# A third raw tile for seven-product pairs, five weight slots instead of six, and another pairing of the product banks

## The chip, the core and the metric

The kernel runs on one core of a Trainium2 chip. The core's engines that matter here are PE (matrix products into PSUM; its weight loads appear as PEld), DVE (elementwise arithmetic), ACT (copies with a change of type, activations) and SP, whose queue issues nearly all the loads from HBM. Each engine works through its own queue in order and waits there for the others by semaphores. The metric is the device time of one execution in microseconds (us), as the median of several runs.

## The reference: what is computed

A decoder trunk of two layers over 256 tokens of width 2048, all in float32. Each layer is a mixer (layer 0: sliding-window attention beside an mLSTM; layer 1: forgetting attention) and a gated feed-forward network (FFN) of hidden width 5632. The change touches the code that computes the FFN:

```python
def swiglu(xn, w_gate, w_up, w_down):
    return (jax.nn.silu(xn @ w_gate) * (xn @ w_up)) @ w_down
...
        h = h + mix.astype(h.dtype)
        h = h + swiglu(rms_norm(h, norm_ffn[layer]), w_gate[layer], w_up[layer], w_down[layer])
```

## The kernel before

**Precision.** A float32 operand is kept as two float32r tiles, `hi` (a rounded copy) and `lo` (what the copy lost). One product of blocks is then three matmuls into one accumulator, `hi`x`hi`, `lo`x`hi`, `hi`x`lo` (`three`, L563 to L565). Activations are split once; weights stream through once and are split on the way. A split of weights is a cast on ACT (L212, L386) and a subtraction on DVE (L213, L387).

**Pair groups.** `pair_group` (L567) multiplies the 256 tokens (two halves `t0`, `t1` of 128) by 512 columns of two weight matrices, or of two column ranges of one matrix. It walks over pairs of k blocks (a k block is 128 rows). A pair is done in one of two ways:

- *plain*: the two matrices' chunks (two k blocks by 512 columns each) are loaded into raw tiles of a pool of four, split into one **slot** each (a `hi` and a `lo` tile of two blocks), and used in 2 x 2 x 2 = 8 products, 24 matmuls.
- *with seven products* (as in Strassen's scheme): all four weight blocks are loaded into one raw tile of four blocks (tag `quad`, two buffers). Three blocks are split as they are into a **triple** (two of these; L648, 128x1536 elements). Then DVE forms differences inside the raw tile (L651, L654, L655), and these are split into two slots (L657 and L658). Seven products, 21 matmuls, follow (L663 to L669); four of them go into the accumulators `prods[0]` to `prods[3]`, three into the plain accumulators.

`ORDER` has eight pairs, of which the second, fourth and sixth are done with seven products. In the FFN a group makes two slots per pair in either way. `slot()` hands out the entries of `stock`, six slots in rotation; a slot is written again once PE has finished with what was in it.

**PSUM.** In the FFN each of two pools, `pa` and `pm`, has two tiles of two banks (a bank holds 128x512 float32). A group's plain accumulators, `plain[0]` and `plain[1]`, are two tiles of one pool and its four products two tiles of the other. The next group changes the pools over (`par`), so that its plain accumulators take the tiles in which the products of this group were.

**The end of a group.** `combine` (L581) adds up the products: ACT copies `prods[0]` (L583), DVE adds `prods[3]` (L585), `prods[2]` (L586) and `prods[1]` (L587, both results at once). Then DVE adds the plain accumulators (L701), ACT and DVE apply the gate (L703, L705), and the result is transposed, by DMA (L734, L736, L741) or, for the last group of the first part, by PE (L720). The outcome is split and summed for the down projection by the function `join` (L387 with `ml`, L300 to L303). The tile `c` that `combine` writes has one buffer, so L583 has to wait until the `join` of the group before has read it.

**The order.** The FFN runs in three parts of 3, 4 and 4 gate/up groups; each part is followed by two groups of the down projection, which adds up over the parts. The order of instructions within each engine's queue is laid out when the program is built, by a simulated time line (`schedule_with_timeline_sim=True`): weight splits of the next group may stand ahead of the end of this one. A tile's buffer is handed on when the last reader of the whole tile is done.

**Around it.** `close_layer` runs the output projection (`out_proj`), sets up the FFN's tiles, takes the `stock` and runs `ffn`. Outside the FFN `stock` is empty and each `slot()` takes fresh tiles of the pool `wp` (tags `hi` and `lo`, six buffers each).

Of the kernel before, what the change touches and what calls it, by code (L numbers as in the profile page):

```python
# [7 lines left out]
F32 = mybir.dt.float32  # L8
BF16 = mybir.dt.bfloat16
F32R = mybir.dt.float32r  # L10
# [7 lines left out]
P = 128  # L18
# [5 lines left out]
NB = 512  # L24
CK = 2
# [29 lines left out]
QUADS = 2  # L55
# [20 lines left out]
def trunk(  # L76
# [24 lines left out]
    mh = sp_.tile([P, KT, S], F32R, name="mh")  # L101
    ml = sp_.tile([P, KT, S], F32R, name="ml")
    wp = ctx.enter_context(tc.tile_pool(name="wp", bufs=6))
    stock, triples = [], []

    def slot():
        if not stock:
            return [wp.tile([P, CK, NB], F32R, tag=a, name=a) for a in ("hi", "lo")]
        stock.append(stock.pop(0))
        return stock[-1]  # L110

    def triple():
        triples.append(triples.pop(0))
# [104 lines left out]
    def two_banks(par, name):  # L218
        return Acc((pm if par else pa).tile([P, NT, NB], F32, tag="pm" if par else "acc", name=name))
# [347 lines left out]
    def pair_group(fp, par, lhs, sums, mats, order, todo=(), halves=None, inner=None, raws=None):  # L567
        plain = [two_banks(par, "acc") for _ in range(2)]
        begun = set()

        def fresh(*at):
            known = at in begun
            begun.add(at)
            return not known

        todo = list(todo)
        prods = None
        kinds = [kind for kind, _ in order]
        t0, t1 = slice(0, P), slice(P, 2 * P)

        def combine(prods):  # L581
            c = fp.tile([P, 4, NB], F32, tag="c", name="c", bufs=1)
            nc.scalar.copy(c[:, 0, :], prods[0])  # L583
            if halves is None:
                nc.vector.tensor_tensor(out=c[:, 1, :], in0=prods[3], in1=c[:, 0, :], op=ALU.add)  # L585
                nc.vector.tensor_tensor(out=c[:, 2, :], in0=prods[2], in1=c[:, 1, :], op=ALU.add)  # L586
                nc.vector.tensor_tensor(  # L587
                    out=c[:, 1:4:2, :],
                    in0=prods[1].rearrange("p (a n) -> p a n", a=1).broadcast_to([P, 2, NB]),
                    in1=c[:, 1:3, :],  # L590
                    op=ALU.add,
                )
                return c
            nc.vector.tensor_tensor(out=c[:, 2, :], in0=prods[3], in1=c[:, 0, :], op=ALU.add)
            nc.vector.tensor_tensor(out=c[:, 1, :], in0=prods[2], in1=c[:, 2, :], op=ALU.add)
            nc.vector.tensor_tensor(out=c[:, 3, :], in0=prods[1], in1=c[:, 1, :], op=ALU.add)
            nc.vector.tensor_tensor(out=c[:, 2, :], in0=prods[1], in1=c[:, 2, :], op=ALU.add)
            return c

        for pos, (kind, pair) in enumerate(order):  # L600
            k0 = 2 * pair
            if inner is not None and pos == len(order) - 1:
                c = combine(prods)
                inner()
            if not kind:
                last = pos == len(order) - 1
                walk = [(i, t) for i in range(CK) for t in range(NT)]
                if last:
                    walk.sort(key=lambda it: it[1])
                for m, (w, c0) in enumerate(mats):  # L610
                    hi, lo = load_chunk(w, k0, c0, NB)
                    run_due(todo, pos)
                    for i, t in walk:
                        ah, al = lhs(k0 + i)
                        ts = slice(t * P, (t + 1) * P)
                        three(
                            plain[m][t], ah[:, ts], al[:, ts], hi[:, i, :], lo[:, i, :],
                            fresh(m, t), last and i == CK - 1,
                        )
                continue  # L620
            first, last = 1 not in kinds[:pos], 1 not in kinds[pos + 1 :]
            if first:
                if 1 - par and halves:
                    prods = [pm.tile([P, NB], F32, tag="pm", name="prod") for _ in range(4)]
                else:
                    prods = [b for _ in range(2) for b in two_banks(1 - par, "prod")]
            if halves:
                ra, rb = (load_raw(w, k0, c0, NB, fp, W_RAWS, raws) for w, c0 in mats)
                hg, lg = split_chunk(ra, NB)
                run_due(todo, pos)  # L630
                hu, lu = (m[:, 0, :] for m in slot())
                split_plain(hu, lu, rb[:, 0, :])
                nc.vector.tensor_tensor(out=ra[:, 1, :], in0=rb[:, 1, :], in1=ra[:, 1, :], op=ALU.subtract)
                nc.vector.tensor_tensor(out=rb[:, 1, :], in0=rb[:, 1, :], in1=rb[:, 0, :], op=ALU.subtract)
                nc.vector.tensor_tensor(out=rb[:, 0, :], in0=rb[:, 0, :], in1=ra[:, 1, :], op=ALU.subtract)
                nc.vector.tensor_tensor(out=ra[:, 0, :], in0=ra[:, 0, :], in1=rb[:, 0, :], op=ALU.subtract)
                parts = []
                for src in (ra, rb):
                    hs, ls = halves.pop(0)
                    halves.append((hs, ls))  # L640
                    split_plain(hs, ls, src)
                    parts += [(hs[:, b, :], ls[:, b, :]) for b in range(CK)]
            else:
                raw = fp.tile([P, 2 * CK, NB], F32, tag="quad", name="raw", bufs=QUADS)
                for m, (w, c0) in enumerate(mats):
                    load_raw(w, k0, c0, NB, into=raw[:, CK * m : CK * (m + 1), :])
                hg, lg = triple()
                latest[0] = split_plain(hg, lg, raw[:, 0:3, :])  # L648
                hu, lu = hg[:, 2, :], lg[:, 2, :]
                run_due(todo, pos)  # L650
                nc.vector.tensor_tensor(  # L651
                    out=raw[:, 1:4:2, :], in0=raw[:, 3:4, :].broadcast_to([P, 2, NB]), in1=raw[:, 1:3, :], op=ALU.subtract
                )
                nc.vector.tensor_tensor(out=raw[:, 2, :], in0=raw[:, 2, :], in1=raw[:, 1, :], op=ALU.subtract)  # L654
                nc.vector.tensor_tensor(out=raw[:, 0, :], in0=raw[:, 0, :], in1=raw[:, 2, :], op=ALU.subtract)  # L655
                (h1, l1), (h0, l0) = slot(), slot()
                split_plain(h1, l1, raw[:, 1:4:2, :])  # L657
                split_plain(h0, l0, raw[:, 0:3:2, :])  # L658
                parts = [((h0, h1)[b % 2][:, b // 2, :], (l0, l1)[b % 2][:, b // 2, :]) for b in range(4)]
            sh, sl = sums(pair)  # L660
            xa, la = lhs(k0)
            xb, lb = lhs(k0 + 1)
            three(prods[0], xb[:, t0], lb[:, t0], hg[:, 1, :], lg[:, 1, :], first, last)  # L663
            three(plain[0][0], xa[:, t0], la[:, t0], hg[:, 0, :], lg[:, 0, :], fresh(0, 0), False)
            three(plain[1][0], sh[3], sl[3], hu, lu, fresh(1, 0), False)
            three(prods[1], sh[0], sl[0], *parts[1], first, last)
            three(prods[2], sh[2], sl[2], *parts[3], first, last)
            three(prods[3], sh[1], sl[1], *parts[2], first, last)
            three(plain[0][1], xa[:, t1], la[:, t1], *parts[0], fresh(0, 1), False)  # L669
        if inner is None:  # L670
            c = combine(prods)
        return plain, c
# [129 lines left out]
    def close_layer(layer, w_out, idx, key, **rest):  # L802
        with tc.tile_pool(name=f"fp{layer}", bufs=2) as fp:
            junk_of[:] = fp, "tmp", 2
            nx = len(mixed_of(ORDER))
            nd = max(len(mixed_of(o)) for o in DOWN.values())
            sx = [fp.tile([P, nx, 4, P], F32R, name=f"sx{i}", bufs=1) for i in range(2)]
            x4 = fp.tile([P, 2, P], F32R, name="x4", bufs=1)
            todo = out_proj(w_out, idx, key, (*sx, x4, fp))
            sd = [fp.tile([P, nd, 4, P], F32R, tag=f"sd{i}", name=f"sd{i}", bufs=1) for i in range(2)]  # L810
            triples.extend([fp.tile([P, 3, NB], F32R, name=f"{a}{i}", bufs=1) for a in ("hi", "lo")] for i in range(2))
            stock.extend([slot() for _ in range(6)])
            renew_pm(2)
            ffn(layer, fp, sx, x4, sd, key, todo, **rest)
            renew_pm(4)
            stock.clear()
            triples.clear()


    acc0 = new_acc()  # L820
    hi, lo = slot()
# [598 lines left out]
```

## Time and profile before

| | us |
|---|---|
| median of 3 runs | 2149.96 |
| lowest and highest run | 2145.96, 2150.37 |
| the profiled execution | 2147.85 |
| its span, first to last instruction | 2146.1 |
| PE busy | 2088.5 (97%) |
| DVE busy | 1801.8 (84%) |
| ACT busy | 1357.8 (63%) |
| mean granted clock of PE | 0.987 |

In the page's groups a line gives: source line, engine, operation, output<-inputs, shape, count | busy time in all, mean ns of one | idle time of the engine just before such instructions, and what ended it. In the view of waits a line gives who waited for whom: us in all, times, longest. In a time line each row has start and length in us, then, in brackets, how long the engine had been idle and what ended that. In the view of windows a row gives, for a stretch of time, each engine's busy time with its count of instructions, the clock granted to PE as a share of full speed, the busy share of the DMA engines and GB/s.

### The profile page before, as it was taken

The numbers are of one execution on the slowest core, as the hardware profiler recorded it, in microseconds if no ns is written. First come the engines' busy times: TensorE is split into PE (matmuls) and PEld (weight loads), VectorE is DVE, ScalarE is ACT, GpSimd is POOL, SyncE is SP. The second block draws the span as 40 slices with busy tenths as digits, with TensorE's granted clock in tenths as the row PEclk, the third lists the DMA queues.
The fourth block names the chain that finished last, engine by engine and source line by source line (L and its number), as shares of the span: only waits on it lengthen the run. The fifth ranks groups of instructions, "written<-read, shape, count | busy, mean of one in ns | idle before, by whom it ended". The sixth has DMA issues, their size and how long they took to land.

```text
span 2146.1 us, 26428 instructions
## 1 busy us (share of the span) xinstructions
PE 2088.5 (97%) x9473; PEld 1726.3 (80%) x9473; DVE 1801.8 (84%) x2095; ACT 1357.8 (63%) x1649; POOL 40.0 (2%) x69
## 2 busy tenths in 40 slices
PE   9999999989999999999999999999999999999997
PEld 7878887868888888787888887888778878888786
DVE  6788779898898999988798777589988889899884
ACT  6766677654666556566676766686654567456563
POOL 1000000000000000000000000000000000000000
PEclk9999999999999999999999999999999999999999
DMA  8666676666676667665676765576756666667663
GB/s 287 181 188 198 201 242 204 203 199 196 209 219 191 206 206 226 215 189 155 209 221 182 224 212 171 168 236 225 226 168 192 219 188 204 210 193 217 199 194 136
DMA packets 309572, 434.84 MB, mean 203 GB/s; under 512 B 106413, under 2 KB 114625, under 8 KB 309313
## 3 DMA queue, kind: packets, MB, share of 16 engines
q1 hardware_dynamic: 307088, 426.27, 63.4%
q0 software_dynamic: 1632, 5.80, 0.8%
q8 instruction: 74, 1.21, 0.2%
q10 hardware_dynamic: 720, 1.09, 0.1%
q14 instruction: 58, 0.47, 0.1%
HBM read 408.68 MB, written 2.12 MB: 191 GB/s over the span
## 4 chain that ended last, share of the span: by engine, by line
PE 77%; DVE 10%; DMA 5%; issue 4%; ACT 4%; SPq 1%; POOL 0%; ACTq 0%; POOLq 0%; DVEq 0%
PE acc L563 16%; PE acc L564 16%; PE acc L565 16%; PE acc L251 5%; PE acc L250 5%; PE acc L252 5%; PE prod L563 4%; PE prod L564 4%; PE prod L565 4%; DVE lo L213 3%; DVE lo L387 2%; DMA raw<-in_w_down_dram 2%; DMA raw<-in_w_up_dram 1%; ACT hi L386 1%; DVE raw L651 1%
## 5 line engine op out<-in xcount | busy, mean ns | idle before, releaser
L212 ACT CAST hi<-raw 128x1024 fp32r<-128x1024 f32 (+3 forms) x561 | 564.5, 1023 | 316.9 <-PE acc L565 141.9
L213 DVE TENSOR_TENSOR lo<-raw,hi 128x1024 fp32r<-128x1024 f32 (+3 forms) x561 | 658.9, 1185 | 125.3 <-ACT hi L212 124.1
L563 PE MATMUL acc<-hi,xh 128*128 128x512 f32 x1320 | 515.1, 393 | 17.2 <-DVE c L586 15.9
L386 ACT CAST hi<-raw 128x1024 fp32r<-128x1024 f32 (+2 forms) x299 | 345.8, 1167 | 273.7 <-PE acc L565 108.1
L564 PE MATMUL acc<-lo,xh 128*128 128x512 f32 x1320 | 517.1, 392 | 0.0
L565 PE MATMUL acc<-hi,xl 128*128 128x512 f32 x1320 | 515.7, 391 | 0.0
L387 DVE TENSOR_TENSOR lo<-raw,hi 128x1024 fp32r<-128x1024 f32 (+2 forms) x299 | 405.9, 1362 | 112.7 <-ACT hi L386 112.3
L563 PEld LDWEIGHTS acc<-hi,xh 128*128 128x128 f32 x1320 | 249.7, 189 | 71.8 <-issue 19.1
L565 PEld LDWEIGHTS acc<-hi,xl 128*128 128x128 f32 x1320 | 249.7, 189 | 52.4
L564 PEld LDWEIGHTS acc<-lo,xh 128*128 128x128 f32 x1320 | 249.8, 189 | 52.1 <-DVE lo L213 0.2
L563 PE MATMUL acc<-hi,mh 128*128 128x512 f32 x466 | 181.7, 393 | 6.1 <-DVE c L586 5.3
L564 PE MATMUL acc<-lo,mh 128*128 128x512 f32 x466 | 182.5, 392 | 1.1 <-DVE lo L213 1.1
L565 PE MATMUL acc<-hi,ml 128*128 128x512 f32 x466 | 182.1, 391 | 0.0
L250 PE MATMUL acc<-hi,mh 128*128 128x512 f32 (+1 forms) x322 | 126.7, 394 | 4.4 <-DVE c L1273 4.4
L251 PE MATMUL acc<-lo,mh 128*128 128x512 f32 (+1 forms) x322 | 126.0, 391 | 0.0
L252 PE MATMUL acc<-hi,ml 128*128 128x512 f32 (+1 forms) x322 | 125.6, 392 | 0.0
L651 DVE TENSOR_TENSOR raw<-raw 128x1024 f32<-128x1024 f32 x95 | 115.6, 1217 | 0.4
L563 PEld LDWEIGHTS acc<-hi,mh 128*128 128x128 f32 x466 | 88.4, 190 | 25.8 <-issue 6.4
L564 PEld LDWEIGHTS acc<-lo,mh 128*128 128x128 f32 x466 | 88.2, 189 | 20.0 <-DVE lo L213 1.7
L565 PEld LDWEIGHTS acc<-hi,ml 128*128 128x128 f32 x466 | 88.2, 189 | 18.5
L250 PE MATMUL acc<-hi,xh 128*128 128x512 f32 (+3 forms) x288 | 100.0, 347 | 3.0 <-DVE c L1273 1.3
L251 PE MATMUL acc<-lo,xh 128*128 128x512 f32 (+3 forms) x288 | 99.5, 345 | 0.8 <-DVE lo L213 0.6
(356 smaller groups left out, 2935.1 us busy)
## 6 DMA issues: line engine op xcount, KB each, us to landing
raw<-in_w_gate_dram SPq DMA_DIRECT2D x176, 512.0 KB, 4.2
raw<-in_w_up_dram SPq DMA_DIRECT2D x176, 512.0 KB, 4.8
raw<-in_w_down_dram SPq DMA_DIRECT2D x176, 512.0 KB, 4.9
raw<-in_w_in_odd_dram SPq DMA_DIRECT2D x88, 512.0 KB, 4.9
raw<-in_w_in_even_dram SPq DMA_DIRECT2D x51, 512.0 KB, 4.9
raw<-in_w_out_even_dram SPq DMA_DIRECT2D x32, 512.0 KB, 4.8
raw<-in_w_out_odd_dram SPq DMA_DIRECT2D x32, 512.0 KB, 4.2
hr<-in_w_in_even_dram SPq DMA_DIRECT2D x12, 512.0 KB, 4.9
```

The costliest lines, as they stand in the source:

```text
L212: latest[0] = nc.scalar.copy(hi[:, k, 0:n], raw[:, k, 0:n])
L213: nc.vector.tensor_tensor(out=lo[:, k, 0:n], in0=raw[:, k, 0:n], in1=hi[:, k, 0:n].bitcast(F32), op=ALU.subtract)
L250: nc.tensor.matmul(o, ah[:, ts], hi, start=(k == 0), stop=False)
L251: nc.tensor.matmul(o, ah[:, ts], lo, start=False, stop=False)
L252: nc.tensor.matmul(o, al[:, ts], hi, start=False, stop=(k == k_all - 1 and cs.stop == n))
L386: cast = nc.scalar.copy(dst_h, src)
L387: nc.vector.tensor_tensor(out=dst_l, in0=src, in1=dst_h.bitcast(F32), op=ALU.subtract)
L563: nc.tensor.matmul(o, ah, hi, start=start, stop=False)
L564: nc.tensor.matmul(o, ah, lo, start=False, stop=False)
L565: nc.tensor.matmul(o, al, hi, start=False, stop=stop)
L651: nc.vector.tensor_tensor(out=raw[:, 1:4:2, :], in0=raw[:, 3:4, :].broadcast_to([P, 2, NB]), in1=raw[:, 1:3, :], op=ALU.subtract)
```

## The change

It does three things, all in the FFN's pair groups. The stock is five slots in place of six, and the buffer so freed becomes a third raw tile for the pairs with seven products, beside the two of tag `quad`. For that, a slot's `hi` and `lo` become the halves of one tile of `wp`. The three raw tiles are held for the whole FFN and handed out in rotation by `quad()`, starting with the one that comes from `wp`. Lastly, the four products are spread over their two PSUM tiles in another way: `prods[0]` with `prods[3]` and `prods[2]` with `prods[1]`, where it was 0 with 1 and 2 with 3.

```diff
     wp = ctx.enter_context(tc.tile_pool(name="wp", bufs=6))
-    stock, triples = [], []
+    stock, triples, quads = [], [], []
 
     def slot():
         if not stock:
-            return [wp.tile([P, CK, NB], F32R, tag=a, name=a) for a in ("hi", "lo")]
+            both = wp.tile([P, 2, CK, NB], F32R, tag="hi", name="hi")
+            return [both[:, a, :, :] for a in range(2)]
         stock.append(stock.pop(0))
         return stock[-1]
+
+    def quad():
+        quads.append(quads.pop(0))
+        return quads[-1]
...
-                    prods = [b for _ in range(2) for b in two_banks(1 - par, "prod")]
+                    (p0, p3), (p2, p1) = two_banks(1 - par, "prod"), two_banks(1 - par, "prod")
+                    prods = [p0, p1, p2, p3]
...
-                raw = fp.tile([P, 2 * CK, NB], F32, tag="quad", name="raw", bufs=QUADS)
+                raw = quad()
...
-            stock.extend([slot() for _ in range(6)])
+            stock.extend([slot() for _ in range(5)])
+            own = wp.tile([P, 2, CK, NB], F32R, tag="hi", name="raw").rearrange("p a k n -> p (a k) n").bitcast(F32)
+            quads.extend([own] + [fp.tile([P, 2 * CK, NB], F32, tag="quad", name="raw", bufs=QUADS) for _ in range(QUADS)])
             renew_pm(2)
             ffn(layer, fp, sx, x4, sd, key, todo, **rest)
             renew_pm(4)
             stock.clear()
             triples.clear()
+            quads.clear()
```

## The prediction

> **What bounds the kernel now.** I read the page's busy shares first, then what PE waited for, then the time lines around its longest waits.
>
> ```profile
> PE 2088.5 (97%) x9473; PEld 1726.3 (80%) x9473; DVE 1801.8 (84%) x2095; ACT 1357.8 (63%) x1649; POOL 40.0 (2%) x69
> ```
>
> ```profile
> PE acc L563 <- DVE c L586: 21.3, 6, 5.3
> ...
> PE prod L563 <- DVE ml L387: 5.7, 1, 5.7
> ...
> PE acc L563 <- DVE c L587: 1.6, 3, 0.8
> ...
> PE acc L564 <- DVE lo L213: 1.1, 1, 1.1
> ```
>
> PE is the bound, and it is idle for 2146.1 - 2088.5 = 57.6 us. The largest share, 21.3 us, is one kind of wait: the first matmul of a group waits for the addition of `prods[2]` (L586), because its accumulator is the PSUM tile that held that product. Waits for plain splits (L213) hardly occur. The time line of PE has the long waits one by one, each with the last matmul before it:
>
> ```profile
> 479.72 0.79 PE L563 MATMUL prod<-hi,sd 128*128 128x512 f32 x1 [5.67 <-DVE ml L387]
> ...
> 901.38 0.39 PE L565 MATMUL acc<-hi,xl 128*128 128x512 f32 x1
> 906.12 0.77 PE L563 MATMUL acc<-hi,xh 128*128 128x512 f32 x1 [4.36 <-DVE c L586]
> ...
> 1191.20 0.47 PE L250 MATMUL acc<-hi,xh 128*128 128x512 f32 x1 [1.30 <-DVE c L1273]
> ...
> 1545.86 0.39 PE L565 MATMUL acc<-hi,xl 128*128 128x512 f32 x1
> 1551.10 0.77 PE L563 MATMUL acc<-hi,mh 128*128 128x512 f32 x1 [4.85 <-DVE c L586]
> ...
> 1743.29 0.39 PE L565 MATMUL acc<-hi,xl 128*128 128x512 f32 x1
> 1748.98 0.77 PE L563 MATMUL acc<-hi,xh 128*128 128x512 f32 x1 [5.30 <-DVE c L586]
> ...
> 2000.62 0.39 PE L565 MATMUL acc<-hi,xl 128*128 128x512 f32 x1
> 2006.23 0.76 PE L563 MATMUL acc<-hi,xh 128*128 128x512 f32 x1 [5.22 <-DVE c L586]
> ```
>
> A long wait costs more than itself. The view of windows sets a stretch without waits beside the one after the wait that ends at 906.12:
>
> ```profile
> 568.00:611.00 43.00, 43.00 (x192) 35.60 (x190) 41.13 (x44) 28.55 (x29) 0.00 (x0) 1.00 0.74 220
> ...
> 906.00:912.00 6.00, 5.88 (x14) 4.65 (x15) 5.86 (x6) 1.71 (x3) 0.00 (x0) 0.50 0.83 317
> ```
>
> At clock 1.00 a matmul takes 43.00/192 = 0.224 us, afterwards, at clock 0.50, 5.88/14 = 0.42. These 14 slow matmuls cost 14 x 0.196 = 2.7 us. The same rows show DVE at 41.13 of 43 us in a gate group: it has hardly more room than PE. After the wait of 1.30 us the first matmul took 0.47 us, after the four long ones 0.76 to 0.77.
>
> Why is L586 late? Before the wait that ends at 1748.98, in the time lines of SP, ACT and DVE:
>
> ```profile
> 1730.48 0.37 SPq L151 DMA_DIRECT2D raw<-in_w_gate_dram  x1
> 1730.90 0.46 SPq L151 DMA_DIRECT2D raw<-in_w_up_dram  x1
> ```
>
> ```profile
> 1731.48 1.06 ACT L212 CAST hi<-raw 128x1024 fp32r<-128x1024 f32 x1 [0.98 <-PE prod L565]
> 1737.48 1.48 ACT L386 CAST hi<-raw 128x1536 fp32r<-128x1536 f32 x1 [4.95 <-DMA raw<-in_w_up_dram]
> ```
>
> ```profile
> 1729.24 1.21 DVE L387 TENSOR_TENSOR lo<-raw,hi 128x1024 fp32r<-128x1024 f32 x1
> ...
> 1739.00 1.76 DVE L387 TENSOR_TENSOR lo<-raw,hi 128x1536 fp32r<-128x1536 f32 x1 [2.39 <-ACT hi L386]
> ...
> 1744.68 0.68 DVE L585 TENSOR_TENSOR c<-prod,c 128x512 f32<-128x512 f32 x1
> ...
> 1748.15 0.68 DVE L586 TENSOR_TENSOR c<-prod,c 128x512 f32<-128x512 f32 x1
> ...
> 1750.49 1.21 DVE L587 TENSOR_TENSOR c<-prod,c 128x1024 f32<-128x1024 f32 x1
> ```
>
> The split that ends at 1729.24 + 1.21 = 1730.45 is the last reader of a four-block raw tile. Only then do the two loads of the next such tile go out, at 1730.48 and 1730.90. ACT, done with its work at 1732.5, stands 4.95 us before that tile's cast, and DVE is idle for 2.39. What ends the group, L585 to L587, is queued behind on both engines.
>
> **The third raw tile.** It lets this load go out one plain pair and one with seven products earlier (45 matmuls of 0.224, 10 us), so the data is there at 1732.5. The cast also needs a free triple, of which there are still two; I take it as free, since PE had begun the pair that used it. The gain is DVE's idle time. The other places, with their own idle times:
>
> ```profile
> 476.70 1.76 DVE L387 TENSOR_TENSOR lo<-raw,hi 128x1536 fp32r<-128x1536 f32 x1 [2.24 <-ACT hi L386]
> ...
> 896.14 1.76 DVE L387 TENSOR_TENSOR lo<-raw,hi 128x1536 fp32r<-128x1536 f32 x1 [1.81 <-ACT hi L386]
> ...
> 901.83 0.68 DVE L585 TENSOR_TENSOR c<-prod,c 128x512 f32<-128x512 f32 x1
> ...
> 907.64 1.21 DVE L587 TENSOR_TENSOR c<-prod,c 128x1024 f32<-128x1024 f32 x1
> ...
> 1545.13 0.68 DVE L585 TENSOR_TENSOR c<-prod,c 128x512 f32<-128x512 f32 x1
> ...
> 1551.47 1.22 DVE L587 TENSOR_TENSOR c<-prod,c 128x1024 f32<-128x1024 f32 x1
> ...
> 1996.25 1.76 DVE L387 TENSOR_TENSOR lo<-raw,hi 128x1536 fp32r<-128x1536 f32 x1 [2.68 <-ACT hi L386]
> ...
> 2001.93 0.68 DVE L585 TENSOR_TENSOR c<-prod,c 128x512 f32<-128x512 f32 x1
> ...
> 2007.74 1.21 DVE L587 TENSOR_TENSOR c<-prod,c 128x1024 f32<-128x1024 f32 x1
> ```
>
> At 1551 DVE was not idle; I count nothing there from this part. At 479.72 the wait falls from 5.67 to 5.67 - 2.24 = 3.4 us.
>
> **The banks.** The next group's first accumulator now takes the tile of `prods[0]` and `prods[3]`, free after L585. With DVE earlier by its idle time, L585 ends at 902.5 - 1.8 = 900.7, 1545.8, 1745.4 - 2.4 = 1743.0 and 2002.6 - 2.7 = 1999.9, each time before PE's last matmul has ended (at 901.8, 1546.3, 1743.7, 2001.0): the first wait is gone. What is late next is the second tile, free after L587, which PE reaches twelve matmuls (2.7 us) into the group. L587 ends at 908.85 - 1.8 = 907.0, 1552.7, 1751.7 - 2.4 = 1749.3, 2008.95 - 2.7 = 2006.3; PE is there at 904.5, 1549.0, 1746.4, 2003.7. So four waits stay: 2.5, 3.7, 2.9 and 2.6, 11.7 us in place of 4.36 + 4.85 + 5.30 + 5.22 = 19.7. Gain 8.0, and 2.2 at 479.72. The two short waits for L586 turn into waits for L587, at no gain. `prods[1]` moves into the later tile, so a group needs that tile three matmuls (0.7 us) sooner; PE has no wait in the whole view for the additions that free it (L701), so this costs nothing, and at most 0.7 us in each of 33 groups.
>
> The slow matmuls: a wait of 1.30 us leaves the clock up, one of 4.36 does not. By the nearer of the two (the middle is 2.8), the waits of 2.5 and 2.6 keep full speed, and 2.9, 3.7 and 3.4 do not: two stretches go, 2 x 2.7 = 5.5 us.
>
> **Five slots.** ACT's casts already wait for PE to leave a slot:
>
> ```profile
>   PE acc L565: 250.0, 154
> ```
>
> (The line is from the raw tiles' list of what ended idle time of the engine ahead of an instruction: us, times.) With five, each cast may start one chunk of twelve matmuls, 2.7 us, later, and its subtraction after it; behind them in ACT's and DVE's queues stand the next casts and the group's end. As a slot's content is ready several chunks ahead of PE, this is hidden in most groups; with that cover gone, one subtraction more falls behind each gate group's end:
>
> ```profile
> L213 DVE TENSOR_TENSOR lo<-raw,hi 128x1024 fp32r<-128x1024 f32 (+3 forms) x561 | 658.9, 1185 | 125.3 <-ACT hi L212 124.1
> ```
>
> There are 22 gate groups, so the bound is 22 x 1.2 = 26 us. At the long waits the sign can turn: a split that has to wait for its slot can no longer stand ahead of L586. Bounds -5 and 26; I take 3 us, nearer to PE's 1.1 us of waits for L213.
>
> **The rest.** The new raw tile comes from the pool that `out_proj` still uses, and it serves the first such pair of each FFN. If it came free only with `out_proj`'s last matmuls, the load would be late: 6.5 us from the issue at 1730.90 to the cast at 1737.48, and the cast itself 1.48. Bounds 0 and 2 x 8 us; I take 1, since PE comes to that pair only after a plain pair. One tile for `hi` and `lo` holds a `lo` one matmul longer, hidden by the cast that has to precede its next writing; nothing. The loads that move ahead in SP's queue let the plain loads behind them go out sooner; nothing.
>
> **Sum**, against the profiled execution: 2147.85 - 8.0 - 2.2 - 5.5 + 3 + 1 = 2136 us. That execution lies 2 us under the median of the runs, within their spread of 4.4 us, so I predict 2136 without correction. Its own range is 2128 to 2144.
>
> **The clock, weighed.** The Trainium skill (TensorE: Matmul & The Clock Gate, Part 1) says that PE's clock falls to half after an idle window of about 3.4 us. The traced waits of 1.30 and 4.36 us agree, and 0.50 is half.
>
> **Rivals.**
> 1. *The clock stays up after every remaining wait* (what the rule just named makes of waits of 2.5 to 3.7 us; no row shown has a wait between 1.30 and 4.36 to contradict it). Then three more slow stretches go: 2136 - 8 = 2128 us. Chance 0.13.
> 2. *The group's end moves up whole.* L583 stood behind the late cast; without it ACT and DVE can have the combination done before PE ends the group. Then the 19.7 and 5.7 us of waits and all five slow stretches go: 2147.85 - 25.4 - 13.5 + 4 = 2113. Against it: DVE is busy for 41 of 43 us, so work moved up pushes other work back. Chance 0.15.
> 3. *Nothing gained from the raw tile:* the cast waits for its triple instead. Then L587 stays where it was, the second waits are 4.4, 3.7, 5.3 and 5.2, and the gain is 1 us: 2147 plus or minus 3. This is the case in which the change doesn't do what it says. For it: casts do wait for PE's products (0.98 us at 1731.48). Chance 0.12.
> 4. *The slot decides, and it is slower.* In every gate group DVE, with 2 us to spare, loses its lead of one split to ACT's longer waits, and PE meets it: +26 us against a gain of 15.7, so 2147.85 + 10 + 1 = 2159. It decides from 15.7/22 = 0.7 us a gate group on. For it: 250 us of such waits now. Chance 0.27.
>
> **Chances.** My forecast has 0.33. Faster by over 0.2% (4.3 us, what a measurement here can tell): 0.33 + 0.13 + 0.15, less a little for the forecast's upper edge, 0.60. Rival 3 and that edge give 0.12 for within 0.2%, rival 4 gives 0.28. The range is 2108 to 2163: rival 2 with 5 us below it, rival 4 with 4 above.
>
> **What would show it.** Right: the 128x1536 casts no longer idle for a load of a raw tile, the waits for L586 are gone, and waits for L587 of 2 to 4 us stand in their place. Rival 1 shows as clock 1.00 after these; rival 3 as idle time of that cast ended by PE; rival 4 as waits of PE for L213, L387 or the casts, and more than 250 us of casts waiting for PE. A wait at the first seven-product pair after either `out_proj` would show my 1 us wrong.

## The result, and the profile after

| | before | after |
|---|---|---|
| median of 4 runs, us | 2148.28 | 2126.01 |
| lowest and highest run | 2145.96, 2150.37 | 2124.25, 2127.69 |
| ratio, with 95% interval | | 0.9897 (0.9879 to 0.9914) |
| profiled execution, and its span | 2147.85, 2146.1 | 2127.0, 2125.3 |
| mean granted clock of PE | 0.987 | 0.995 |

The change makes the kernel 22 us faster (1.0%). That is inside the whole range, 2108 to 2163, which holds every rival, but beyond the likeliest value, 2136, and 2 us below the range that the forecast itself was given, 2128 to 2144. The executions that were profiled differ by 20.8 us of span. Lines of the code have moved: in the profile of after, L568 to L570 are `three`, L590, L591 and L592 the additions of `prods[3]`, `prods[2]` and `prods[1]`, L217 and L218 the plain splits, L391 and L392 the other splits. A slot's `lo` now has the name `hi`, since both are one tile.

The page's busy times of after:

```profile
PE 2080.8 (98%) x9473; PEld 1716.2 (81%) x9473; DVE 1800.0 (85%) x2095; ACT 1365.9 (64%) x1649; POOL 40.8 (2%) x69
```

PE is idle for 2125.3 - 2080.8 = 44.5 us where it was 57.6: 13.1 of the 20.8 us are idle time, and the other 7.7 are PE's busy time. That 7.7 is a balance. By the starts of the matmuls in the two time lines, against 0.227 us from one to the next, before loses 17 us in seven slow stretches, each after a wait of 4 us or more, and after loses 4 in two. The short waits, of which after has more, take some 5 us of this back, since the matmuls beside a short wait count longer than 0.227 us. The view of waits of after (us in all, times, longest) says which waits these were:

```profile
PE prod L568 <- DVE xl L398: 6.0, 1, 6.0
PE acc L255 <- DVE c L1282: 5.4, 2, 4.5
PE prod L568 <- DVE ml L392: 4.4, 2, 2.2
PE acc L568 <- ACT hi L217: 2.8, 7, 0.7
PE prod L569 <- DVE hi L392: 2.5, 3, 1.7
PE prod L568 <- ACT hi L391: 2.3, 3, 1.4
PE prod L568 <- issue: 1.8, 1, 1.8
PE acc L569 <- DVE hi L218: 1.5, 2, 0.8
...
PE acc L568 <- DVE c L592: 1.2, 2, 0.6
```

The waits for the combination were 21.3 us for `prods[2]` and 1.6 for `prods[1]`. What is left is 1.2 us, all of it for `prods[1]`. Not one long wait stands at the start of a gate group. The list is now led by two waits that are not in the gate groups at all: the end of layer 0 (L398) and the mixer of layer 1 (L255).

The second half of the argument is the raw tile. Groups by form, for the 128x1536 cast (busy, mean ns | idle time of ACT ahead of it, and what ended it), of before and of after:

```profile
L386 ACT CAST hi<-raw 128x1536 fp32r<-128x1536 f32 x95 | 140.8, 1482 | 100.2 <-DMA raw<-in_w_up_dram 34.3 <-PE prod L565 30.7 <-PE acc L565 18.3
```

```profile
L391 ACT CAST hi<-raw 128x1536 fp32r<-128x1536 f32 x95 | 140.9, 1484 | 68.0 <-PE prod L570 30.3 <-PE acc L570 28.3 <-DMA raw<-in_w_up_dram 8.5
```

ACT's idle time ahead of these casts that ended with the load of `w_up` falls from 34.3 to 8.5 us. What these lines do not name falls from 16.9 to 0.9 (in before it is nearly all the load of `w_down`: ACT's list for L386 has 16.6 for it). What PE ends (a triple or a slot comes free) grows from 49.0 to 58.6, and the sum falls by 32.

How far the end of a group has moved up shows in the group whose first matmul stood at 2006.23 before, after a wait of 5.22 us. By the count of matmuls its first one is now that at 1987.81. The time lines of DVE and of PE of after:

```profile
1985.97 1.22 DVE L592 TENSOR_TENSOR c<-prod,c 128x1024 f32<-128x1024 f32 x1
```

```profile
1976.02 0.39 PE L570 MATMUL prod<-hi,sx 128*128 128x512 f32 x1
...
1987.58 0.39 PE L570 MATMUL acc<-hi,xl 128*128 128x512 f32 x1
1987.81 0.39 PE L568 MATMUL acc<-hi,xh 128*128 128x512 f32 x1
```

and the last product and the first matmul behind it in the same group of before:

```profile
1992.24 0.39 PE L565 MATMUL prod<-hi,sx 128*128 128x512 f32 x1
1992.46 0.39 PE L564 MATMUL acc<-lo,xh 128*128 128x512 f32 x1
```

All three additions are done at 1987.19, before PE comes to the next group; the pairing of the banks has nothing to do there. One part of this had not been thought of: PE's own order, which is laid out with the rest, is another one in this group. The last product starts 1987.81 - 1976.02 = 11.8 us before the next group, where it was 2001.0 - 1992.24 = 8.8 us before the group's end. That leaves ACT and DVE 3 us more for the combination. It is not so everywhere: in the groups that waited at 1551.10 and 1748.98 the distance was 8.8 us and is 9.0 and 9.1, and the wait is gone there too.

### The profile page after: what moved, and what is told of

It is laid out like the page before. It is cut to its first block, busy times and chain, and to the rows that moved or that the text cites. A ratio compares the mean times of both kernels' runs of the same rounds, so it can differ in the third digit from the quotient of the medians.

```text
span 2125.3 us, 26400 instructions
## 1 busy us (share of the span) xinstructions
PE 2080.8 (98%) x9473; PEld 1716.2 (81%) x9473; DVE 1800.0 (85%) x2095; ACT 1365.9 (64%) x1649; POOL 40.8 (2%) x69
## 4 chain that ended last, share of the span: by engine, by line
PE 80%; DVE 6%; ACT 5%; DMA 4%; issue 3%; SPq 1%; POOL 0%; ACTq 0%; POOLq 0%; DVEq 0%
PE acc L569 18%; PE acc L570 18%; PE acc L568 18%; PE prod L569 4%; PE prod L568 4%; PE prod L570 4%; PE acc L255 4%; PE acc L256 4%; PE acc L257 4%; DVE hi L218 2%; ACT hi L217 1%; DMA raw<-in_w_up_dram 1%; ACT box L356 1%; ACT hi L391 1%; DMA raw<-in_w_in_odd_dram 1%
## 5 line engine op out<-in xcount | busy, mean ns | idle before, releaser
L217 ACT CAST hi<-raw 128x1024 fp32r<-128x1024 f32 (+3 forms) x561 | 569.7, 1025 | 388.4 <-PE acc L570 244.0
L218 DVE TENSOR_TENSOR hi<-raw,hi 128x1024 fp32r<-128x1024 f32 (+3 forms) x561 | 660.5, 1187 | 131.6 <-ACT hi L217 130.6
L570 PE MATMUL acc<-hi,xl 128*128 128x512 f32 x1320 | 513.6, 389 | 0.0
L568 PE MATMUL acc<-hi,xh 128*128 128x512 f32 x1320 | 508.8, 391 | 3.5 <-ACT hi L217 2.1
L391 ACT CAST hi<-raw 128x1024 fp32r<-128x1024 f32 (+2 forms) x299 | 347.0, 1170 | 249.9 <-PE acc L570 184.0
L569 PE MATMUL acc<-hi,xh 128*128 128x512 f32 x1254 | 489.0, 390 | 1.5 <-DVE hi L218 1.5
L568 PEld LDWEIGHTS acc<-hi,xh 128*128 128x128 f32 x1320 | 247.8, 188 | 58.9 <-ACT hi L217 6.9
L570 PEld LDWEIGHTS acc<-hi,xl 128*128 128x128 f32 x1320 | 247.8, 188 | 51.4
L569 PEld LDWEIGHTS acc<-hi,xh 128*128 128x128 f32 x1254 | 235.4, 188 | 52.0 <-DVE hi L218 3.4
L392 DVE TENSOR_TENSOR hi<-raw,hi 128x1024 fp32r<-128x1024 f32 (+1 forms) x204 | 240.8, 1183 | 29.3 <-ACT hi L391 29.2
L392 DVE TENSOR_TENSOR lo<-raw,hi 128x1536 fp32r<-128x1536 f32 x95 | 166.7, 1755 | 71.5 <-ACT hi L391 67.6
L570 PE MATMUL acc<-hi,ml 128*128 128x512 f32 x466 | 181.5, 390 | 0.0
L568 PE MATMUL acc<-hi,mh 128*128 128x512 f32 x466 | 178.2, 389 | 0.7 <-ACT hi L217 0.7
L569 PE MATMUL acc<-hi,mh 128*128 128x512 f32 x437 | 170.2, 390 | 0.1
L255 PE MATMUL acc<-hi,mh 128*128 128x512 f32 (+1 forms) x322 | 127.1, 395 | 4.5 <-DVE c L1282 4.5
L256 PE MATMUL acc<-hi,mh 128*128 128x512 f32 (+1 forms) x322 | 126.2, 392 | 0.0
L657 DVE TENSOR_TENSOR raw<-raw 128x1024 f32<-128x1024 f32 x95 | 115.8, 1219 | 0.1
L568 PEld LDWEIGHTS acc<-hi,mh 128*128 128x128 f32 x466 | 87.5, 188 | 19.2 <-ACT hi L217 1.1
L255 PE MATMUL acc<-hi,xh 128*128 128x512 f32 (+3 forms) x288 | 100.1, 347 | 2.2 <-DVE c L1282 0.9
L570 PEld LDWEIGHTS acc<-hi,ml 128*128 128x128 f32 x466 | 87.5, 188 | 18.1
L256 PE MATMUL acc<-hi,xh 128*128 128x512 f32 (+3 forms) x288 | 99.4, 345 | 0.8 <-DVE hi L218 0.6
```

The lines of the kernel that those rows point to most:

```text
L217: latest[0] = nc.scalar.copy(hi[:, k, 0:n], raw[:, k, 0:n])
L218: nc.vector.tensor_tensor(out=lo[:, k, 0:n], in0=raw[:, k, 0:n], in1=hi[:, k, 0:n].bitcast(F32), op=ALU.subtract)
L255: nc.tensor.matmul(o, ah[:, ts], hi, start=(k == 0), stop=False)
L256: nc.tensor.matmul(o, ah[:, ts], lo, start=False, stop=False)
L391: cast = nc.scalar.copy(dst_h, src)
L392: nc.vector.tensor_tensor(out=dst_l, in0=src, in1=dst_h.bitcast(F32), op=ALU.subtract)
```

## The experiments

Three theories. **A**: the raw tile that is in time made the gain. **B**: the pairing of the banks made it. **C**: any small edit lays the order of the queues out anew, and the time of this kernel moves by such amounts without a reason. Medians are over 4 to 11 runs; the ratio is to the kernel before on the same chip, with its 95% interval.

**1. The banks alone** (six slots, two raw tiles):

```diff
-                    prods = [b for _ in range(2) for b in two_banks(1 - par, "prod")]
+                    (p0, p3), (p2, p1) = two_banks(1 - par, "prod"), two_banks(1 - par, "prod")
+                    prods = [p0, p1, p2, p3]
```

> Before with the new pairing of the product banks alone (six slots, two raw tiles). Theory A, the raw tile made the gain: the waits for L586 go, but the next group's second accumulator waits for L587 instead, 4 to 5 us at the same four places; 2144 to 2149 us. Theory B, the banks made it: 2126 to 2135 us and no long wait at a group's start.

Measured: 2134.79 us, ratio 0.994 (0.9926 to 0.9953). From its view of waits:

```profile
PE acc L563 <- ACT mh L386: 7.7, 5, 3.3
...
PE acc L563 <- DVE c L585: 3.5, 2, 2.4
...
PE acc L563 <- DVE c L587: 2.9, 3, 2.0
```

The pairing does what its description says: the 21.3 us for `prods[2]` are gone, with 3.5 us for `prods[3]` and 2.9 for `prods[1]` in their place. The waits for `mh`, most of them in the down projection, grow from 0.3 to 7.7 us. The time is not the 2144 to 2149 us that went with A: the pairing alone is worth 13 us, at the upper edge of what went with B. So this run by itself does not part the two theories.

**2. The raw tile and five slots, with the old pairing** (the change without the two lines above).

> The changed kernel with the old pairing of the banks (five slots, three raw tiles). Theory A: the combination is done before PE ends the group, so it does not matter which bank comes free first; 2125 to 2130 us, no wait of 4 us for the combination. Theory B: the long waits for the addition of the third product are back; 2136 us or more.

Measured: 2125.43 us, ratio 0.9899 (0.9884 to 0.9915): the whole gain. Its waits for `prods[2]` (L591 here):

```profile
PE acc L568 <- DVE c L591: 6.7, 2, 3.4
```

Two are left, each of 3.36 us, of six. So B falls as the cause of the whole gain: with the raw tile in time the pairing adds nothing to the time, and what it saves in these waits is lost elsewhere.

**3. Five slots alone** (two raw tiles, old pairing):

```diff
-            stock.extend([slot() for _ in range(6)])
+            stock.extend([slot() for _ in range(5)])
```

> Before with five slots in place of six and nothing else (two raw tiles, old banks). The price of the slot alone. If the cover holds, as the prediction took it: 2149 to 2154 us. If the slot decides (the rival that was slower): up to 26 us more, about 2170 us, with waits of PE for splits in most gate groups.

Measured: 2137.36 us, ratio 0.9952 (0.994 to 0.9965). Neither time that was expected came; the kernel is faster with a buffer less, by half of the whole gain. From its waits and the raw tiles' list of what ended the idle time of the engine ahead:

```profile
PE acc L563 <- DVE c L586: 12.1, 4, 4.5
...
PE prod L564 <- DVE lo L387: 4.4, 5, 1.4
```

```profile
  PE acc L565: 339.2, 198
```

ACT waits longer for slots (339 us in place of 250), and PE waits 12.1 us for `prods[2]` in place of 21.3. The prediction named a way in which the sign could turn: a split that has to wait for its slot no longer stands ahead of the combination. The numbers fit that, but no run took it apart, so it stays an argument, and the cause of these 11 us is open.

**4. The new raw tile handed out last** in place of first:

```diff
-            quads.extend([own] + [fp.tile(...) for _ in range(QUADS)])
+            quads.extend([fp.tile(...) for _ in range(QUADS)] + [own])
```

> The changed kernel with the raw tile from the slots' pool handed out third instead of first. If the new waits at the first seven-product pair of each FFN (about 3 to 4 us each) come from that tile being freed late by the output projection: 2118 to 2122 us, and the first 128x1536 cast of each FFN long before PE needs it. If they come from the five slots: 2126 us as the changed kernel.

Measured: 2125.12 us, ratio 0.9906 (0.9892 to 0.9919). It is aimed at the start of the FFN. In after, loads, cast and matmuls of the first seven-product pair, in the time lines of SP, ACT and PE:

```profile
320.39 1.18 SPq L156 DMA_DIRECT2D raw<-in_w_up_dram  x2
```

```profile
328.92 1.47 ACT L391 CAST hi<-raw 128x1536 fp32r<-128x1536 f32 x1 [3.22 <-DMA raw<-in_w_up_dram]
```

```profile
330.44 0.50 PE L568 MATMUL prod<-hi,xh 128*128 128x512 f32 x1 [1.37 <-ACT hi L391]
336.12 0.50 PE L568 MATMUL acc<-hi,xh 128*128 128x512 f32 x1 [0.62 <-ACT hi L217]
337.38 0.50 PE L569 MATMUL acc<-hi,xh 128*128 128x512 f32 x1 [0.76 <-DVE hi L218]
...
360.92 0.50 PE L569 MATMUL prod<-hi,sx 128*128 128x512 f32 x1 [0.40 <-DVE hi L392]
```

These four waits are 3.2 us, and the second FFN has their like at 1418.99 to 1449.00 (1.80, 0.23, 0.77, 0.39). With the tile handed out last, the first three of each are gone (the FFNs' first waits for a split are 0.78 us at 358.57 and 1.44 at 1445.64). The time is that of after all the same, so neither expectation holds whole: the waits go, as in the first, and the time stays, as in the second. From its view of waits:

```profile
PE prod L568 <- DVE xl L398: 6.3, 1, 6.3
...
PE acc L568 <- ACT mh L391: 3.6, 2, 2.7
PE pf L726 <- DVE ml L392: 2.3, 1, 2.3
```

The 6.3 us at the end of layer 0 were there before (6.0 in after). New are some 3.3 us for `mh` (0.3 in after) and 2.3 us ahead of the transposes (L726). The profiled execution, 2128.90 us, is slower than the median of this run, so these sizes are rough.

**5 to 7. Is it luck of the order?** Two edits of before that change nothing of what is late, and one of them on after: `hi` and `lo` of a fresh slot as halves of one tile (5), and 12 dummy matmuls at the program's start in place of 9, in before (6) and in after (7).

```diff
-            return [wp.tile([P, CK, NB], F32R, tag=a, name=a) for a in ("hi", "lo")]
+            both = wp.tile([P, 2, CK, NB], F32R, tag="hi", name="hi")
+            return [both[:, a, :, :] for a in range(2)]
```

```diff
-COLD = 9
+COLD = 12
```

> Before with a slot's hi and lo as halves of one tile and nothing else (six slots, two raw tiles, old banks). It moves no work and frees nothing sooner. Theory A (each part acts by the wait that it removes): 2144 to 2152 us, the four long waits for L586 as before. Theory C (any change that makes the queues be laid out anew shakes the long waits off): clearly below 2144 us.

> Before with 12 in place of 9 warm-up matmuls at the very start (under 1 us of PE time that waits for the first data anyway). A probe of the order alone: the queues are laid out anew, no buffer changes. Theory A: 2145 to 2151 us. Theory C: below 2144 us, other places and lengths of the long waits, with casts of 128x1536 still waiting some 50 us for their raw tile.

> The same probe on the changed kernel. If the changed kernel owes its time to three raw tiles: 2122 to 2130 us in this order too, and under 15 us of waits of 128x1536 casts for their raw tile. If it owes it to a lucky order: above 2132 us, with waits of 4 us or more for the combination at group starts.

Measured: 2146.73 us, ratio 0.9992 (0.9983 to 1.0001); 2144.83 us, ratio 0.9981 (0.9972 to 0.999); 2126.69 us, ratio 0.9897 (0.9884 to 0.9911). Runs 5 and 7 came as theory A had it. Run 6 lies between the two expectations, 0.2 us below A's; PE's waits for `prods[2]` are still 23.1 us in it (21.6 in run 5). Such edits move the time by 0 to 4 us (5 in run 10 below), far less than 22, and after keeps its gain. C falls for the whole change; differences of up to 5 us between the kernels here should not be read.

**8. Five slots and the new banks, without the raw tile** (the edits of 1 and 3 on before):

```diff
-            stock.extend([slot() for _ in range(6)])
+            stock.extend([slot() for _ in range(5)])
...
+                    (p0, p3), (p2, p1) = two_banks(1 - par, "prod"), two_banks(1 - par, "prod")
```

> Before with five slots and the new banks, still two raw tiles: what the changed kernel is without its raw tile. Theory A: the casts wait some 50 us for raw tiles again, and the time is between that of five slots alone (2137.4) and that of the changed kernel (2126.0), 2130 to 2137 us. If the raw tile adds nothing to the other two parts: 2126 us or less.

Measured: 2166.84 us, ratio 1.0081 (1.0068 to 1.0095): slower than before, and 41 us slower than after, from which only the raw tile (and with it the joining of `hi` and `lo`, worth nothing in run 5) is missing. Neither expectation saw this. Each of the two edits alone had gained 10 to 13 us. The view of waits, and the form of the cast:

```profile
PE acc L564 <- DVE lo L387: 11.0, 5, 2.8
PE prod L563 <- DVE xl L393: 9.8, 1, 9.8
PE acc L564 <- DVE lo L213: 7.1, 8, 1.5
...
PE acc L563 <- ACT hi L212: 4.8, 7, 1.2
...
PE prod L564 <- DVE lo L387: 2.9, 2, 1.5
```

```profile
L386 ACT CAST hi<-raw 128x1536 fp32r<-128x1536 f32 x95 | 140.8, 1482 | 91.0 <-DMA raw<-in_w_up_dram 36.7 <-PE prod L565 29.3 <-DMA raw<-in_w_down_dram 24.7
```

Here PE meets the splits, as in the prediction's rival 4: 11.0 + 7.1 + 4.8 + 2.9 = 26 us of waits for them, where run 3 has 7.0 for the same kinds (4.4 + 2.6). With 9.8 us at the end of layer 0 they make more than half of PE's idle time, 2165.1 - 2097.3 = 67.8 us, which is 23.3 us above after's. PE's busy time is 16.5 us above after's, with slow stretches after several of these waits. The casts lose 61 us to loads of their raw tile (some 51 in before). But rival 4 gave longer waits of ACT for slots as the reason, and these are 283 us here, less than the 339 of run 3, which gained. Why the new pairing turns the gain of run 3 into a loss is open.

**9 and 10. The kernels of 1 and 8 laid out anew**: the banks alone (9), and five slots with the new banks (10), each with

```diff
-COLD = 9
+COLD = 12
```

> The new banks alone (six slots, two raw tiles) with 12 warm-up matmuls: another order of the same kernel. If the 2134.8 us of the new banks alone come from the banks: 2131 to 2139 us again. If they were a lucky order of the queues: 2142 us or more.

> Five slots and the new banks with two raw tiles, with 12 warm-up matmuls. If the 2166.8 us come from these buffers (casts late for their raw tile, with one slot less to cover it): 2160 to 2172 us and again some 25 us of PE waiting for splits. If it was an unlucky order: below 2150 us.

Measured: 2134.2 us, ratio 0.9944 (0.9932 to 0.9956), and 2161.73 us, ratio 1.007 (1.0057 to 1.0083). Gain and loss stay, within 5 us.

**11. Four slots**, with three raw tiles and the new banks (after with):

```diff
-            stock.extend([slot() for _ in range(5)])
+            stock.extend([slot() for _ in range(4)])
```

> The changed kernel with four slots instead of five (three raw tiles). How much cover the slots leave once the raw tile is in time. If the fifth slot is spare: 2124 to 2132 us. If the cover is used up: 2145 us or more, PE waiting for casts and subtractions of weights (L217, L218, L392) by some 1 us a gate group.

Measured: 2121.04 us, ratio 0.9876 (0.9863 to 0.9889). In its raw tiles' list ACT waits 399.6 us for PE to leave a slot (after: 428.0), and its longest waits of PE for splits are

```profile
PE prod L568 <- ACT hi L391: 5.0, 4, 2.7
...
PE acc L569 <- DVE hi L218: 2.1, 4, 1.2
PE acc L568 <- ACT hi L217: 2.0, 4, 1.1
```

The time is below what was expected, not above. With the raw tile in time, the fifth slot buys nothing either.

**12. Three raw tiles, five slots, the old banks, the new tile handed out last** (the kernel of 2 with the edit of 4):

```diff
-            quads.extend([own] + [fp.tile(...) for _ in range(QUADS)])
+            quads.extend([fp.tile(...) for _ in range(QUADS)] + [own])
```

> Three raw tiles, five slots, the old banks, and the tile from the slots' pool handed out last: an attempt at a better version. If the waits at the start of each FFN can be had back without new ones: 2119 to 2123 us. If they turn up elsewhere, as with the new banks: 2124 to 2128 us.

Measured: 2119.75 us (2117.94 to 2123.29), ratio 0.9876 (0.9863 to 0.9888). With 11 it is the fastest of the kernels run; its highest run is below the lowest of after (2124.25), but the two intervals overlap. The time came as expected, the reason did not: the waits for splits at the start of the two FFNs are 4.3 us in all against 4.8 in run 2, at other places. What the 6 us against run 2 come from is not shown.

The parts together, in us (medians):

| | old banks | new banks |
|---|---|---|
| two raw tiles, six slots | 2148 (before) | 2134.8 |
| two raw tiles, five slots | 2137.4 | 2166.8 |
| three raw tiles, five slots | 2125.4 | 2126.0 (after) |

Read down the columns, the raw tile is worth 12 us with the old banks and 41 with the new. Read along the rows, the banks are worth -13, +29 and +1. No run has three raw tiles beside six slots, so the raw tile was not tried alone. Nor was one rival run: the raw tiles are now held for the whole FFN and no longer taken afresh for each pair. By the code this frees nothing sooner. Each of the last two splits of a tile (L657, L658) reads a block of either half, so the loads of both halves have to wait for the later of the two, as they did before, and in before the first load went out 0.03 us after it (1730.45 and 1730.48).

## Why the prediction was right, and where it was not

**The number: in part luck.** The sum took 8.0 us off for the combination and 5.5 for the clock, where 21.7 and 7.7 came off, and put 4 on for new waits, where some 10 came on. So the forecast was 14 us short in the first, and the 6 us that it lacked in the last hid nearly half of that.

**The raw tile: right in its mechanism.** The cast no longer stands for its load (34.3 to 8.5 us ended by `w_up`). Run 2 shows that the gain is whole without the banks, run 8 that the other two parts without the tile are a loss. How much is the tile's own is less clear: with the old banks five slots alone already give 11 of the 22 us (run 3), and the tile adds 12.

**The banks: the step that failed.** It reads "So four waits stay: 2.5, 3.7, 2.9 and 2.6, 11.7 us in place of 4.36 + 4.85 + 5.30 + 5.22 = 19.7." The runs show none of the four; 22.9 us of waits for L586 and L587 became 1.2. The forecast moved L587 up by DVE's own idle time and left everything else in its place. But the late cast held back a queue, and the combination stood in it: with the cast in time, all additions are done before PE needs the tile, but for two waits of 0.6 us, and in some groups the products end earlier in PE's order too. That is the mechanism of rival 2, the group's end moved up whole, which had a chance of 0.15; its 2113 us were not reached, for the reasons below. The banks then add nothing to the time: run 2 has the old pairing and the same time, though two of its waits for `prods[2]` are left. Where the raw tile was late (run 1), the step was nearer: the waits for L586 went, and waits for L585 and L587 came, 6.4 us in all and none above 2.4, but the time fell by 13 us and not by a few.

**The wait at 479.72** was to fall from 5.67 to 3.4; it is 2.20 and 1.67 now, in all 3.9. Its like in layer 1 is new (2.23 us).

**The slow clock: the price right, the count wrong.** The sum had two stretches go, 5.5 us. All five went, which follows from the step before: of the seven waits of 4 us or more in before, two are left (6.02 and 4.51 us). The five stretches cost 2.4 to 3.0 us each, 13.7 in all, as rival 2 had it (13.5). That PE's busy time fell by no more than 7.7 comes from the short waits, which were in no sum: they take some 5 us back. Rival 1's condition could not show, since the waits that it speaks of are gone; by the rule that it names, the wait of 3.7 us, longer than 3.4, could have gone either way.

**The slots: near by luck.** Three us were taken, within -5 and 26. After has 4.3 us of waits for plain splits (L217 and L218) where 1.1 was, 3.2 more. But 2.4 of the 4.3 stand at the start of the FFNs, where the order of the raw tiles makes them (run 4), and a slot has no price of its own: one fewer is -11 us alone, +32 with the new banks and two raw tiles, and with three raw tiles about -5 (run 11, whose interval overlaps that of after); the first two lie outside the bounds. The sign that was named for rival 4, more than 250 us of casts that wait for a slot, came (428 us) without its loss. So long waits of casts for slots are no evidence of a loss; PE's waits for splits are.

**The layer's start: too small.** One us was taken, within 0 and 16. The four waits of each FFN are 3.2 us, 6.4 in all. Run 4 shows both that the order of the tiles makes most of them and that taking them away gains nothing: other waits come up, those for `mh` and ahead of the transposes.

**Not in the sum:** the end of layer 0, where PE waited 4.02 and 1.15 us and now 6.02. DVE has the raw tiles' differences and splits for the next weights ahead of the last `xl` there (L398).

Put together for the profiled execution: 2147.85 less 21.7 (combination), 1.8 (479.72) and 7.7 (clock), and with 2.2 (1568.27), 3.2 (plain splits), 4.0 (the rest of the starts, L391, L392 and the wait for issue, 1.37 + 0.40 + 1.80 + 0.39) and 0.9 (layer 0's end) is 2127; the waits left out cancel to within 0.2 us. Against rival 2's 2113 that is 14 us more: 6 from the clock, 6 from the new waits and 4 at 479.72, less 2, since the short waits for the combination went too.

## What to carry to other kernels

A wait for a buffer can cost more than itself when other work stands behind it in the queue. Here a load that came late held a cast, and behind the cast stood work that belonged to another stage; the wait that the profile blamed was that of the last of them. To size such a repair, ask not by how much the blamed instruction moves but whether anything still holds it once the queue flows. And parts that help alone can hurt together: two gains of 10 and 13 us gave a loss of 17 here (by the ratios of runs 3, 1 and 8), so a change in several parts is tested part by part and in pairs.

## What the runs showed of the hardware

Between 2 and 3 us it is not the length of a wait alone that decides on the clock. The kernel of run 8 has two waits of the same length, in the time line of PE:

```profile
917.84 0.60 PE L564 MATMUL acc<-lo,xh 128*128 128x512 f32 x1 [2.42 <-DVE lo L387]
...
1529.83 0.50 PE L564 MATMUL acc<-lo,xh 128*128 128x512 f32 x1 [2.42 <-DVE lo L387]
```

and in the view of windows (the clock is the third number from the end) the four us after each of them:

```profile
917.80:921.80 4.00, 3.96 (x10) 3.15 (x11) 4.00 (x5) 0.00 (x0) 0.00 (x0) 0.57 0.86 285
1529.80:1533.80 4.00, 3.97 (x17) 3.30 (x18) 4.00 (x5) 0.00 (x0) 0.00 (x0) 1.00 0.91 307
```

After the first PE ran 10 matmuls at a clock of 0.57, after the second 17 at 1.00. In after, the waits of 2.20 and 2.23 us left the clock up (1.00 over the four us after each); the nine waits of 4 us or more in before and after were all followed by a slow stretch. The four us after the wait of 2.20 us and after that of 6.02:

```profile
480.00:484.00 4.00, 3.54 (x14) 2.47 (x14) 4.00 (x6) 1.81 (x2) 0.00 (x0) 1.00 0.26 96
1010.40:1014.40 4.00, 4.00 (x10) 3.13 (x11) 0.00 (x0) 1.05 (x1) 0.00 (x0) 0.50 0.00 0
```

So the prediction's middle of 2.8 us was no threshold, and rival 1's 3.4 was none either: the clock fell after 2.42. The Trainium skill (TensorE: Matmul & The Clock Gate, Part 1) says that the activity window of about 3.4 us is free-running, and that the point at which the clock changes depends on where in the window the first matmul lands. The two equal waits with different outcomes agree with that, though no run shows the window itself. The same page's table of the two states has the half clock come after at least one idle window of about 3.4 us; the drop after a wait of 2.42 us does not agree with a window that is wholly idle.
